# A down projection in seven products instead of eight

## The chip, the cores and the metric

The kernel runs on one core of a Trainium2 chip. A core has TensorE (matrix products, into the PSUM banks), VectorE (DVE), ScalarE (ACT), GpSimd (POOL) and SyncE (SP, which here issues the transfers), each with its own queue, and 16 DMA engines. The metric is the time of one execution on the device in microseconds (us), lower is better. The profile is one execution taken by the hardware profiler.

## The reference

One layer of a streaming encoder for 1024 + 64 = 1088 tokens of width 1024, in float32: token mixers, cross attention, an MLP and a last norm.

```python
x += mix @ w_out
x += cross_attention(rms_norm(x), mem_k, mem_v)
h = rms_norm(x, norm_ffn_g)
x += square(relu(h @ w_up)) @ w_down      # w_up 1024 x 4096, w_down 4096 x 1024
y = rms_norm(x, final_g)
```

This case is about the last two lines. With t = square(relu(h @ w_up)), the down projection multiplies t (1088 x 4096) by w_down and adds the result to x.

## The kernel before

Activations lie transposed, with features on the 128 partitions and tokens along the free axis. A feature block is 128 features, so x has 8, t has 32. To keep float32 accuracy at the faster matmul format, every operand is split into a high part (ACT copies it to the format fp32r) and a low part (DVE subtracts), and each product is three matmuls: high x high, high x low, low x high (`mm3`). `tt` is a two-input operation on DVE, or on POOL where asked; `split_lo` makes the low part.

The **up projection** (`up`) already uses seven products. Two output blocks, the two halves of the inner dimension and the two quarters of a token half form a 2 x 2 x 2 problem; seven products of sums of these (named "1" to "7", done in the order "1562734") replace eight, each of 4 inner blocks x 3 matmuls of 272 columns. A job is one pair of output blocks for one token half (84 matmuls) or both (168). `self.jobs` lists three one-half jobs, thirteen with both halves, and three one-half jobs for the half left out at the start (`LATE = 3`). `pair_units` forms the sums of weights on POOL and splits them; the results of a job are rectified, squared, scaled and stored to a DRAM buffer (`tdram`).

The **down projection** is plain. The 32 blocks of t are taken in eight groups of four (`FBS`); the next group is loaded (`t_load`) and split (`t_split`) while this one is multiplied. For each of the 8 output blocks and each of three token groups, 4 x 3 matmuls go to one PSUM bank, and DVE adds the bank to the residual tile `xr` in SBUF. So every one of the eight groups adds into all of `xr`. The last group is taken by token groups of 416, 416 and 256, each followed by its final norm and stores.

Buffers: 35 slots of 1152 columns shared by nearly everything, three each for raw, high and low weights, eight PSUM banks in two tags of four. Up to the end of the attention a helper (`inorder`) keeps each engine's operations in written order; in the MLP the framework's planner places an operation when by its own estimate its inputs and a buffer are there, in written order among those that are ready. A queue then executes what it was given strictly in order.

Of the kernel before, what the change touches and what calls it, by code (L numbers as in the profile page):

```python
# [23 lines left out]
FB = 4  # L24
NFB = 32 // FB
# [3 lines left out]
NSLOT = 35  # L29
# [11 lines left out]
LATE = 3  # L41
FBS = list(range(2, NFB)) + [1, 0]
# [11 lines left out]
class Trunk:  # L54
    def __init__(self, nc, tc, a, pools):
        self.nc, self.tc, self.a = nc, tc, a
        self.const, self.wp, self.sp, self.tp, self.ps, self.dp = pools
        self.uid = 0
        self.bg = []
        self.seq = {}  # L60
        self.hold = None
        self.consts()
# [11 lines left out]
    def bank(self, tag):  # L74
        return self.ps.tile([P, 512], F32, tag=tag, name=self.name("ps" + tag))
# [5 lines left out]
    def consts(self):  # L81
# [10 lines left out]
        self.masks = c.tile([P, 8, 512], U8, name="masks")  # L92
# [905 lines left out]

    def pair_units(self):

        gp = self.nc.gpsimd
        (_, ri), (_, rj) = self.raws.pop(0), self.raws.pop(0)
        s12, s34 = (self.slot(n="sw")[:, :1024].rearrange("p (k n) -> p k n", k=KT) for _ in range(2))
        self.tt(s12[:, :4], rj[:, :4], rj[:, 4:], ADD, gp)
        self.tt(s12[:, 4:], s12[:, :4], ri[:, :4], SUB, gp)
        self.tt(s34[:, :4], ri[:, :4], rj[:, :4], SUB, gp)
        self.tt(s34[:, 4:], ri[:, 4:], s12[:, 4:], SUB, gp)
        ops = {}
        for src, k0, names in ((ri, 0, "12"), (s12, 0, "56"), (s34, 0, "73"), (rj, 4, "4")):
            hi = self.wp.tile([P, KT, P], F32R, tag="whi", name=self.name("wh"))  # L1010
            lo = self.wp.tile([P, KT, P], F32R, tag="wlo", name=self.name("wl"))
            n = 4 * len(names)
            self.act(hi[:, :n], src[:, k0:k0 + n], AF.Copy)
            self.split_lo(lo[:, :n], src[:, k0:k0 + n], hi[:, :n])
            for j, x in enumerate(names):
                ops[x] = (hi[:, 4 * j:4 * j + 4], lo[:, 4 * j:4 * j + 4])
            if names == "4":
                self.fetch()
                self.fetch()
# [5 lines left out]
    def up(self, ops, units, ready, tdram, side):  # L1025


        jobs = self.jobs
        for n, (p, cs) in enumerate(jobs):
# [3 lines left out]
            for i, m in enumerate(self.ORDER):  # L1033
# [23 lines left out]
                if m in "5273":  # L1057
# [4 lines left out]
                    elif m in "73":  # L1062
                        self.prep()
                if i < len(steps):
                    steps[i]()
            del ops[:4]
            for c in cs:
                self.nc.sync.dma_start(tdram[2 * p:2 * p + 2, :, c * H:c * H + H].rearrange("o p t -> p o t"), st[c][1])

    def mlp(self, o, x1, x2src):  # L1070
        nc = self.nc
        tdram = self.dp.tile([4 * NFB, P, T], F32, name="tt")
        self.jobs = [(p, (0,)) for p in range(LATE)] + [(p, (0, 1)) for p in range(LATE, NPAIR)]
        self.jobs += [(p, (1,)) for p in range(LATE)]
        self.halves, self.accs = [[], []], []
        ready = [{}, {}]
        self.rb = self.two(n="rb")
# [9 lines left out]
        def first():  # L1087
# [5 lines left out]
        unit = lambda: ops.append(next(units))  # L1093
        self.project(0, o[0], x1, x2src, {5: [a], 6: [a, first], 7: [a]})
        self.project(1, o[1], x1, x2src, {0: [a, ra], 1: [ra, a], 2: [a], 3: [a], 4: [a], 5: [a, b], 6: [b, unit],
                                          7: [b, unit]})
        xr, raws, ts = [], {}, {}

        def t_load(fb):
            raws[fb] = []  # L1100
            for f in range(FB):
                t = self.slot(n="t")
                nc.sync.dma_start(t[:, :T], tdram[FB * fb + f])
                raws[fb].append(t)

        def t_split(fb):
            ts.setdefault(fb, []).append(self.hl(raws[fb].pop(0)[:, :T], None))

        def xr_load():
            x = self.slot(n="xr")  # L1110
            nc.sync.dma_start(x[:, :T], x2src[len(xr)])
            xr.append(x)
        f0 = FBS[0]
        sp = lambda: t_split(f0)
        self.up(ops, units, ready, tdram, {
# [232 lines left out]
```

## Time and profile before

| what | value |
|---|---|
| median of 3 runs (lowest, highest) | 1589.76 us (1585.19, 1591.19) |
| profiled execution, its own time | 1591.52 us |
| span of the profile | 1589.7 us |
| PE busy | 1546.3 us (97%) |
| DVE, ACT, POOL busy | 899.9, 578.4, 225.3 us |
| mean granted TensorE clock | 0.982 |

The span is the time from the first to the last instruction. A busy engine sets the time only where others wait for it, so the stretches have to be looked at one by one. Lines name the engine, the line of the code, the operation and the tiles as output<-inputs: `wl<-wr,wh` is the low part of a weight from its raw and high part, `xr<-psd,xr` the addition of a bank to the residual.

### The profile page before, as it was taken

The numbers are of one execution on the slowest core, as the hardware profiler recorded it, in microseconds if no ns is written. First come the engines' busy times: TensorE is split into PE (matmuls) and PEld (weight loads), VectorE is DVE, ScalarE is ACT, GpSimd is POOL, SyncE is SP. The second block draws the span as 40 slices with busy tenths as digits, with TensorE's granted clock in tenths as the row PEclk, the third lists the DMA queues.
The fourth block names the chain that finished last, engine by engine and source line by source line (L and its number), as shares of the span: only waits on it lengthen the run. The fifth ranks groups of instructions, "written<-read, shape, count | busy, mean of one in ns | idle before, by whom it ended". The sixth has DMA issues, their size and how long they took to land.

```text
span 1589.7 us, 24469 instructions
## 1 busy us (share of the span) xinstructions
PE 1546.3 (97%) x10312; PEld 1510.8 (95%) x10312; DVE 899.9 (57%) x1268; ACT 578.4 (36%) x1034; POOL 225.3 (14%) x143
## 2 busy tenths in 40 slices
PE   7899999999999999999998999999989999999997
PEld 7699998899999999989998999999989999999997
DVE  7837868955654433584479444444476444434434
ACT  7711141436252221463455444444353112102124
POOL 2720002200000000000026322222320000000005
PEclk9899999999999999998999999999999999999999
DMA  8421000101013411212542322322376322221103
GB/s 303 160 81 41 27 31 17 36 20 44 28 45 130 153 50 66 80 54 85 177 143 94 108 107 97 110 102 92 108 274 238 124 97 97 72 78 55 53 1 113
DMA packets 54942, 150.60 MB, mean 95 GB/s; under 512 B 6704, under 2 KB 14384, under 8 KB 54832
## 3 DMA queue, kind: packets, MB, share of 16 engines
q1 hardware_dynamic: 51952, 148.37, 26.7%
q8 instruction: 81, 1.33, 0.4%
q10 hardware_dynamic: 2880, 0.66, 0.2%
q14 instruction: 29, 0.24, 0.1%
HBM read 115.11 MB, written 33.91 MB: 94 GB/s over the span
## 4 chain that ended last, share of the span: by engine, by line
PE 64%; issue 26%; DVE 5%; POOL 2%; ACT 1%; DMA 1%; SPq 0%; POOLq 0%; ACTq 0%; DVEq 0%
PE psd L199 46%; PE psm L199 11%; PE psm L536 3%; DVE wl L133 1%; POOL xr L132 1%; DVE cacc L136 1%; POOL sw L132 1%; DMA wr<-w_up 1%; PE psm L614 1%; ACT wh L125 1%; PE psm L616 0%; PE psm L507 0%; DMA wr<-wk 0%; PE psm L625 0%; PE psd L856 0%
## 5 line engine op out<-in xcount | busy, mean ns | idle before, releaser
L199 PE MATMUL psd<-lo,wh 128*128 128x364 f32 (+2 forms) x1632 | 540.6, 331 | 4.2 <-DVE lo L136 4.2
L199 PE MATMUL psd<-hi,wl 128*128 128x364 f32 (+2 forms) x1632 | 541.4, 332 | 3.0 <-DVE wl L133 3.0
L199 PE MATMUL psd<-hi,wh 128*128 128x364 f32 (+2 forms) x1632 | 541.0, 332 | 0.0
L125 ACT ACTIVATE wh<-wr 128x1024 fp32r<-128x1024 f32 (+1 forms) x141 | 138.3, 983 | 495.9 <-PE psd L199 335.1
L199 PEld LDWEIGHTS psd<-lo,wh 128*128 128x128 f32 x1632 | 309.0, 189 | 5.8 <-DVE lo L136 5.5
L199 PEld LDWEIGHTS psd<-hi,wl 128*128 128x128 f32 x1632 | 309.4, 190 | 3.6 <-DVE wl L133 3.2
L199 PEld LDWEIGHTS psd<-hi,wh 128*128 128x128 f32 x1632 | 309.4, 190 | 1.1
L133 DVE TENSOR_TENSOR wl<-wr,wh 128x1024 fp32r<-128x1024 f32 (+1 forms) x141 | 178.1, 1266 | 149.3 <-ACT wh L125 149.3
L133 DVE TENSOR_TENSOR xr<-psd,xr 128x364 f32<-128x364 f32 (+3 forms) x192 | 102.0, 534 | 177.2 <-PE psd L199 177.2
L199 PE MATMUL psm<-th,wh 128*128 128x272 f32 x448 | 131.6, 294 | 4.6 <-ACT wh L125 3.8
L199 PE MATMUL psd<-th,wl 128*128 128x272 f32 x448 | 130.6, 293 | 3.5 <-DVE wl L133 3.5
L199 PE MATMUL psd<-th,wh 128*128 128x272 f32 x448 | 131.0, 293 | 3.0 <-DVE t L133 3.0
L199 PE MATMUL psm<-tl,wh 128*128 128x272 f32 x448 | 130.1, 291 | 0.0
L199 PE MATMUL psm<-th,wl 128*128 128x272 f32 x448 | 130.1, 292 | 0.0
L199 PE MATMUL psd<-tl,wh 128*128 128x272 f32 x448 | 129.9, 290 | 0.0
L199 PEld LDWEIGHTS psm<-th,wh 128*128 128x128 f32 x448 | 85.5, 191 | 5.8 <-ACT wh L125 4.2
L136 DVE SCALAR_TENSOR_TENSOR cacc<-glu,vecs,cacc 128x1118 f32<-128x1118 f32 x60 | 90.5, 1509 | 0.7
L199 PEld LDWEIGHTS psd<-th,wl 128*128 128x128 f32 x448 | 85.4, 191 | 3.7 <-DVE wl L133 3.7
L199 PEld LDWEIGHTS psd<-th,wh 128*128 128x128 f32 x448 | 85.3, 191 | 3.8 <-DVE t L133 3.7
L199 PEld LDWEIGHTS psm<-tl,wh 128*128 128x128 f32 x448 | 85.7, 191 | 0.0
L199 PEld LDWEIGHTS psd<-tl,wh 128*128 128x128 f32 x448 | 85.6, 191 | 0.0
L199 PEld LDWEIGHTS psm<-th,wl 128*128 128x128 f32 x448 | 85.3, 191 | 0.0
(238 smaller groups left out, 2375.9 us busy)
## 6 DMA issues: line engine op xcount, KB each, us to landing
wr<-w_up SPq DMA_DIRECT2D x38, 512.0 KB, 3.3
tt<-t SPq DMA_DIRECT2D x32, 544.0 KB, 2.9
t<-tt SPq DMA_DIRECT2D x32, 544.0 KB, 4.6
wr<-w_down SPq DMA_DIRECT2D x32, 512.0 KB, 3.3
wr<-w_in SPq DMA_DIRECT2D x22, 512.0 KB, 3.2
x<-res SPq DMA_DIRECT2D x16, 544.0 KB, 2.8
wr<-xo SPq DMA_DIRECT2D x16, 512.0 KB, 3.5
x<-xT SPq DMA_DIRECT2D x8, 544.0 KB, 6.6
```

Source lines behind the costliest of these rows:

```text
L125: return self.inorder("act", lambda: self.nc.scalar.activation(out, in_, f, **kw))
L132: return self.inorder("pool", lambda: eng.tensor_tensor(out, a, b, op))
L133: return self.inorder("dve", lambda: self.nc.vector.tensor_tensor(out, a, b, op))
L136: return self.inorder("dve", lambda: self.nc.vector.scalar_tensor_tensor(out, in0, s, in1, op0, op1))
L199: return self.inorder("pe", lambda: self.nc.tensor.matmul(*args, **kw))
L536: mm(pv[:m, c], k[:, c * P:c * P + m], qc[:, :, 1, :], start=True, stop=True)
L614: mm(ps[:w, c * P:c * P + P], sc[:w, s:s + w], vt[:w, s:s + P], start=True, stop=first)
```

## The change

Down becomes a 2 x 2 x 2 problem as well. The two quarters of a token half, two output blocks and the two halves of the inner blocks are combined; seven products per combination. For each token half, four blocks of four pairs of inner blocks; in each, two groups (`dp`) of two pairs of output tiles, so that one product is 2 x 4 x 3 matmuls of 272 columns into two banks. Each of the seven products is followed by one DVE addition of 2 x 272 columns into `xr`.

The sums of t that the products need are made in the up stage: after every job POOL forms four differences of quarters for each half, and they are stored beside t. `t_load` fetches one operand at a time, already summed. The sums of w_down are made on POOL (four of 1024 columns per group), for each token half anew, so w_down is read twice. Five of seven operand splits are on DVE, two on POOL. The first half's final norm runs during the second half's first two blocks. The PSUM pool is closed after up and opened again as four tiles of two banks. `LATE` goes from 3 to 4 (20 jobs, 12 of them with both halves), the slots from 35 to 36, and the weight sums of up are written partly over the raw weights.

```diff
-LATE = 3
+LATE = 4
...
+    def pair_sums(self):
...
         self.tt(s12[:, :4], rj[:, :4], rj[:, 4:], ADD, gp)
         self.tt(s12[:, 4:], s12[:, :4], ri[:, :4], SUB, gp)
-        self.tt(s34[:, :4], ri[:, :4], rj[:, :4], SUB, gp)
-        self.tt(s34[:, 4:], ri[:, 4:], s12[:, 4:], SUB, gp)
+        self.tt(rj[:, :4], ri[:, :4], rj[:, :4], SUB, gp)
+        return ri, rj, s12
...
-                self.nc.sync.dma_start(tdram[2 * p:2 * p + 2, :, c * H:c * H + H].rearrange("o p t -> p o t"), st[c][1])
+                t = st[c][1].rearrange("p o (h t) -> p (o h) t", h=2)
+                self.nc.sync.dma_start(tdram[c, p, :, 0:4], t)
+                d = self.slot(n="d")[:, :4 * Q].rearrange("p (k t) -> p k t", k=4)
+                self.tt(d[:, 0], t[:, 1], t[:, 0], SUB, gp)
+                self.tt(d[:, 2], t[:, 3], d[:, 0], SUB, gp)
+                self.tt(d[:, 1], t[:, 3], t[:, 1], SUB, gp)
+                self.tt(d[:, 3], t[:, 2], d[:, 2], SUB, gp)
+                self.nc.sync.dma_start(tdram[c, p, :, 4:8], d)
...
+    def t_split(self, blk, m):
...
+        self.act(hi, full, AF.Copy)
+        self.tt(lo, full, hi.bitcast(F32), SUB, self.nc.gpsimd if m in "34" else None)
...
+    def quads(self):
...
+                a11, a21 = get(0), get(2)
+                yield
+                a22, a12 = get(3), get(1)
+                yield
+                s1, s2 = (self.slot(n="sw")[:, :1024].rearrange("p (k n) -> p k n", k=KT) for _ in range(2))
+                self.tt(s1, a21, a22, ADD, gp)
+                self.tt(s2, s1, a11, SUB, gp)
+                yield
+                self.tt(a21, a11, a21, SUB, gp)
...
+    def down_units(self):
...
+            for m, src in zip(self.ORDER, (a11, s1, s2, a12, a21, a12, a22)):
...
+                self.act(hi, src, AF.Copy)
+                self.split_lo(lo, src, hi)
+                if m == "2":
+                    self.tt(a12, a12, s2, SUB, self.nc.gpsimd)
+                yield hi, lo
...
+    def down(self, q, loads, splits):
+        units = self.down_units()
+        ops = [next(units), next(units)]
...
+        self.swap_psum()
+        fin = [self.final(c) for c in range(2)]
+        for n, blk in enumerate(self.blocks):
...
+            for dp in range(2):
...
+                    for (a, i, k) in ((0, 0, 0), (0, 0, 1), (0, 2, 2), (0, 4, 3), (0, 6, 4), (1, 2, 5), (1, 3, 6)):
+                        if a == dp:
+                            add(i, self.t_load, nx, self.ORDER[k])
+                    for (a, i, k) in ((0, 2, 0), (0, 4, 1), (0, 6, 2), (1, 0, 3), (1, 2, 4), (1, 4, 5), (1, 6, 6)):
+                        if a == dp:
+                            add(i, self.t_split, nx, self.ORDER[k])
...
+                if n in (NFB, NFB + 1):
+                    for i in range(7):
+                        add(i, next, fin[0], None)
...
+                for i in (0, 1, 3, 4):
+                    add(i, next, q, None)
...
+                for i, m in enumerate(self.ORDER):
...
+                    for pr in range(2):
+                        for k in range(4):
+                            self.mm3(banks[b][:, pr, :Q], wh[:, 4 * pr + k], wl[:, 4 * pr + k], th[:, k], tl[:, k],
+                                     k == 0 and m in "152", k == 3, skip_group_check=m not in "152")
+                    r, h = self.C_AT[m]
+                    x = self.xr[c, dp, r][:, :, h * Q:h * Q + Q]
+                    self.tt(x, banks[b][:, :, :Q], x, ADD)
+                    u = next(units, None)
...
+                    for f in steps[i]:
+                        f()
...
+    def swap_psum(self):
+        self.psx.__exit__(None, None, None)
+        self.psx = self.tc.tile_pool(name="psum2", bufs=4, space=bass.MemoryType.PSUM)
+        self.ps = self.psx.__enter__()
```

Here `mm3` and `split_lo` are unchanged. In `down`, at each product, one further weight unit is split (two products ahead of its use), then the steps listed for that product are done: operand loads and splits for the next block, loads and sums of the next group's weights.

More of the change, by code (lines that the diff above doesn't have):

```diff
@@ L23 @@
 PH = 15
-FB = 4
-NFB = 32 // FB
+NFB = 4
 EPS = 1e-6
@@ L1025, in up @@
     def up(self, ops, units, ready, tdram, side):
-        jobs = self.jobs
-        for n, (p, cs) in enumerate(jobs):
+        gp = self.nc.gpsimd
+        for n, (p, cs) in enumerate(self.jobs):
             cur = ops[0]
@@ L1093, in mlp @@
         unit = lambda: ops.append(next(units))
+        sums = lambda: self.sums.append(self.pair_sums())
         self.project(0, o[0], x1, x2src, {5: [a], 6: [a, first], 7: [a]})
[L1095 to L1104, printed above, removed]
@@ new lines, in mlp @@
+        self.project(1, o[1], x1, x2src, {0: [a, ra], 1: [ra, a], 2: [a], 3: [a], 4: [a], 5: [a, sums], 6: [unit],
+                                          7: [unit, b]})
+        self.blocks = [(c, fb) for c in range(2) for fb in range(NFB)]
+        self.xr = {}
+        self.tq = {}
+        b0 = self.blocks[0]
+        load = [lambda m=m: self.t_load(b0, m) for m in self.ORDER]
+        split = [lambda m=m: self.t_split(b0, m) for m in self.ORDER]
+        x = lambda: self.xr_load(0)
+        q = self.quads()
@@ new lines, in mlp @@
+        qs = lambda: next(q)
+        self.up(ops, units, ready, self.tdram, {
+            0: [[rbb], [b], [rbb], [], [b]], 1: [[b], [], [], [b]], 2: [[b], [], [], [b]],
+            3: [[b], [], [b]],
+            NPAIR: [[load[0]], [], [load[1]], [], [split[0]]],
+            NPAIR + 1: [[load[2]], [], [split[1]], [], [load[3]], [], [split[2]]],
+            NPAIR + 2: [[load[4]], [], [split[3]], [x], [x], [split[4]]],
+            NPAIR + 3: [[x], [x, qs], [qs], [qs], [qs]]})
+        self.down(q, load[5:], split[5:])
@@ new lines, in final @@
+    def final(self, c):
+        nc, gp = self.nc, self.nc.gpsimd
+        accs = []
+        last = c == 1
+        for dp in range(2):
+            sq = [self.two(n="fsq") for _ in range(2)]
+            for r in range(2):
+                self.act(sq[r], self.xr[c, dp, r], AF.Square)
+            self.tt(sq[0], sq[0], sq[1], ADD, None if last else gp)
+            accs += [sq[0][:, 0], sq[0][:, 1]]
+            for r in range(2):
+                for q in range(2):
+                    if not last or r:
+                        x = self.xr[c, dp, r][:, q]
+                        self.act(x, x, AF.Copy, scale=self.vec("final_g", 4 * dp + 2 * q + r))
+            yield
+        r = self.rstd_cols(accs, CT, D, "q")
+        yield
+        ps = self.bank2().rearrange("p a b -> p (a b)")
+        self.bcast_cols(ps, r, CT, 0)
+        rb = self.two(n="frb")[:, 0]
+        self.act(rb, ps[:, :H], AF.Copy)
+        yield
+        for dp in range(2):
+            for r in (1, 0):
+                x = self.xr[c, dp, r]
+                for q in range(2):
+                    o = 4 * dp + 2 * q + r
+                    if last and r == 0:
+                        self.stt(x[:, q], x[:, q], self.vec("final_g", o), ps[:, :H], MUL, MUL)
+                    else:
+                        self.tt(x[:, q], x[:, q], rb, MUL, gp)
+                    nc.sync.dma_start(self.a["o_yT"][o][:, c * H:c * H + H], x[:, q])
+                yield
@@ L1207, in all_weights @@
                 yield "s", a["w_up"][2 * p + j]
-        for fb in FBS:
-            for o in range(4):
-                yield "c", a["w_down"][fb, o]
     def run(self):
```

199 lines of the change are left out of this document (96 added, 103 removed).

## The prediction

> **What bounds the kernel now.** I read the page first, then the busy time by stretch, then the queue of transfers for the pace of one round, then the groups by shape.
>
> ```profile
> span 1589.7 us, 24469 instructions
> PE 1546.3 (97%) x10312; PEld 1510.8 (95%) x10312; DVE 899.9 (57%) x1268; ACT 578.4 (36%) x1034; POOL 225.3 (14%) x143
> DVE  7837868955654433584479444444476444434434
> POOL 2720002200000000000026322222320000000005
> PEclk9899999999999999998999999999999999999999
> ```
>
> TensorE is busy nearly all the time; VectorE and GpSimd look idle over most of the MLP (slices 21 to 40). The stretches of the MLP are: two-half jobs of the up projection, its last three one-half jobs, seven down blocks, the last down block with the end, and (last two rows) the first three one-half jobs of the up projection and the first of them by itself.
>
> ```profile
> 895.00:1145.00 250.00, 250.00 (x1985) 250.00 (x1984) 116.28 (x164) 104.90 (x192) 71.79 (x48) 1.00 0.29 103
> 1152.40:1193.20 40.80, 36.23 (x256) 34.98 (x255) 29.96 (x33) 22.38 (x35) 10.07 (x6) 0.92 0.77 276
> 1192.30:1526.50 334.20, 334.20 (x2018) 334.20 (x2018) 157.48 (x228) 61.66 (x61) 0.00 (x0) 1.00 0.27 97
> 1526.50:1589.70 63.20, 55.16 (x338) 53.52 (x336) 29.37 (x55) 26.38 (x51) 21.10 (x19) 0.94 0.20 71
> 838.00:880.00 42.00, 35.46 (x253) 34.41 (x253) 39.33 (x36) 24.52 (x40) 29.08 (x16) 0.92 0.30 103
> 840.00:862.00 22.00, 17.19 (x112) 16.59 (x111) 21.75 (x17) 12.16 (x21) 19.50 (x11) 0.84 0.21 74
> ```
>
> The columns are length, then busy time and count of PE, weight load, DVE, ACT and POOL, then clock, DMA share and GB/s. In the up jobs and the seven down blocks TensorE is never idle, so matmul time sets the pace, and in the down blocks POOL does nothing at all. The last row is the opposite: DVE is busy 21.75 of 22.00 us, POOL 19.50, and it is TensorE that waits. That row matters below.
>
> **The pace of a matmul.** Transfers repeat once per round:
>
> ```profile
> 942.21 2.58 SPq L1068 DMA_DIRECT2D tt<-t  x2
> 963.40 2.58 SPq L1068 DMA_DIRECT2D tt<-t  x2
> 1254.90 24.22 SPq L159 DMA_DIRECT2D wr<-w_down  x3
> 1302.69 24.22 SPq L159 DMA_DIRECT2D wr<-w_down  x3
> ```
>
> An up job with both halves takes 963.40 - 942.21 = 21.19 us for 2 x 7 x 4 x 3 = 168 matmuls of 272 columns, 0.1261 us each. A down block takes 47.79 us for 8 x 3 x 4 x 3 = 288 matmuls of 364 or 360 columns, 0.1659 us each.
>
> **What the change removes.** Down loses its 8 x 288 = 2304 matmuls and gets 2 halves x 4 blocks x 2 output groups x 7 products x 24 = 2688 of 272 columns, the form of the up jobs. One half block (one output group) is 168 x 0.1261 = 21.2 us on TensorE, a product 3.03 us, and all sixteen are 339 us against 8 x 47.79 = 382. If TensorE alone counts, 43 us are gained.
>
> **What it adds to DVE and POOL.** The durations:
>
> ```profile
> L133 DVE TENSOR_TENSOR xr<-psd,xr 128x364 f32<-128x364 f32 x108 | 57.3, 535 | 97.1 <-PE psd L199 97.1
> L133 DVE TENSOR_TENSOR t<-psm,t 128x272 f32<-128x272 f32 x35 | 15.5, 442 | 21.9 <-PE psm L199 21.9
> L133 DVE TENSOR_TENSOR lo<-t,hi 128x1088 fp32r<-128x1088 f32 x28 | 35.4, 1285 | 5.5 <-ACT hi L125 5.5
> L133 DVE TENSOR_TENSOR wl<-wr,wh 128x1024 fp32r<-128x1024 f32 x27 | 33.0, 1224 | 7.8 <-ACT wh L125 7.8
> L125 ACT ACTIVATE hi<-t 128x1088 fp32r<-128x1088 f32 x28 | 29.5, 1101 | 52.4 <-PE psd L199 47.9 <-DMA t<-tt 4.5
> L125 ACT ACTIVATE wh<-wr 128x1024 fp32r<-128x1024 f32 x27 | 28.6, 1058 | 199.8 <-PE psd L199 199.8
> L136 DVE SCALAR_TENSOR_TENSOR t<-t,rb 128x544 f32<-128x544 f32 x47 | 35.0, 744 | 0.8
> 41.89 2.35 DVE L133 TENSOR_TENSOR wl<-wr,wh 128x1024 fp32r<-128x1024 f32 x2
> ```
>
> Back to back, a weight split takes 2.35/2 = 1.17 us on DVE; an operand split 1.25 by the same small overlap; an addition of two 272-column banks into the residual 0.70 (from 442 ns at 272 columns and 535 at 364, about 1 ns a column: 0.72 at 544). A block of two output groups has 14 weight splits (before: 4), 14 additions and 5 of the 7 operand splits on DVE: 14 x 1.17 + 5 x 1.25 + 14 x 0.70 = 32.4 us in the 42.4 us of TensorE. ACT has 14 x 1.06 + 7 x 1.10 = 22.5 us, which stays hidden. DVE too would be hidden, were it alone. But POOL, idle here before, now gets 8 sums of 1024 columns and two operand splits of 1088 per block. What happens when DVE and POOL work together is seen early in the kernel:
>
> ```profile
> 21.76 2.55 POOL L132 TENSOR_TENSOR sq<-sq,sq 128x1088 f32<-128x1088 f32 x1 [20.79 <-ACT sq L125]
> 50.62 24.60 POOL L132 TENSOR_TENSOR x<-x,rb 128x1088 f32<-128x1088 f32 x7 [14.13 <-ACT rb L125]
> 53.04 9.30 DVE L133 TENSOR_TENSOR wl<-wr,wh 128x1024 fp32r<-128x1024 f32 x3 [1.17 <-ACT wh L125]
> 62.26 3.63 DVE L136 SCALAR_TENSOR_TENSOR lo<-x,vecs,hi 128x1088 fp32r<-128x1088 f32 x1
> 65.82 3.50 DVE L133 TENSOR_TENSOR wl<-wr,wh 128x1024 fp32r<-128x1024 f32 x1
> 845.50 0.78 DVE L133 TENSOR_TENSOR t<-psd,t 128x272 f32<-128x272 f32 x2
> ```
>
> Seven POOL multiplies take 24.60 us, 3.51 each instead of 2.55, and a DVE weight split among them 3.50 instead of 1.17. They take turns: 3.51 is one operation of each. So a 1088-column POOL operation holds up a DVE operation with two SBUF inputs by 3.51 - 1.2 = 2.3 us, and one of 1024 columns by 2.16. The additions from PSUM are not held up (0.78 for two, in the stretch of the last row above where POOL was busy).
>
> The Trainium skill, "SBUF — State Buffer", section "Who interferes with whom", calls this an exclusive lock under which the loser fully blocks; by that a turn would be 2.55 + 1.17 = 3.72 us, which is 0.2 us more than the trace has and would add about 2 us a block (14 us in all) to the sum; I go by the trace.
>
> So a block has 14 x 1.17 + 5 x 1.25 = 22.6 us of such work on DVE and 8 x 2.16 + 2 x 2.3 = 21.9 on POOL. That is 44.5 us if everything else fits beside it, and 54.3 if the 9.8 us of additions never run beside POOL; TensorE needs 42.4. Between them I take 49.4: of ten POOL operations about seven start right behind a weight split that an addition follows (14 of the 19 splits), and each such addition, 0.70 us, runs beside POOL: 54.3 - 4.9. Laid out in order, a half block gives the same: the difference a12 - s2 follows the split of the fourth product's weights, the three sums for the next group take turns with the splits behind it, the sixth split ends 18.0 us into the half block, TensorE had been done with the fifth product at 15.2, and the half block ends after 24.4 us. This lies near the stretch 840 to 862, where DVE is full and TensorE has 17.19 of 22.00.
>
> Down then is 7 blocks x 49.4 = 345.8, and the last block, without next operands and nearly without sums, 42.4. The two POOL splits of the first block fall at its start (2 x 2.3, less 1.0 beside additions: 3.6), and the first half's closing norm puts 2 additions of 1088 and 8 products of 544 on POOL (2 x 2.3 + 8 x 1.15 = 13.8, less 4.9: 8.9) into the fifth and sixth block. The end, once the last product is done, by rows of this size: addition 0.7, square 1.1, sum 1.3, column sums and roots 2.1, reciprocals 0.4, spreading 1.4, copy 0.6, four POOL products of 544 columns 5.5, last store 2.5, together 15.6. Sum 416.3 us. Before, the same stretch was 1589.70 - 1192.30 = 397.4. So **+18.9 us**; its ends are -15.4 (44.5 a block) and +59 (54.3, nothing beside POOL).
>
> **The up stage.** POOL gets four differences of 272 columns per half and job, and SP a second store that waits for them; behind that store stand the next weights, asked for half a job later, so I price no wait there. In a two-half job DVE has 4.2 us of weight splits, 2.6 of rectifying (744 ns rows) and 2.3 of additions, and is held up by four sums and eight differences:
>
> ```profile
> 819.68 1.29 POOL L132 TENSOR_TENSOR sw<-wr,wr 128x512 f32<-128x512 f32 x1
> 842.15 2.27 POOL L132 TENSOR_TENSOR sw<-wr,wr 128x512 f32<-128x512 f32 x1
> 844.39 2.32 POOL L132 TENSOR_TENSOR sw<-sw,wr 128x512 f32<-128x512 f32 x1
> ```
>
> 844.39 - 842.15 = 2.24 us per turn, less 1.2 of DVE, is 1.05 for 512 columns and about 0.6 for 272: 4.2 + 4.8 on top of 9.1 is 18.1 of 21.2 us, hidden. A one-half job has 10.6 us of TensorE and 6.6 + 4.2 + 2.4 = 13.2 on DVE, 2.6 too many, and there are now eight such jobs, not six. The last ones also carry five operand splits (6.3) and the first sums for down (8.6), less 4.2 as the very last job prepares no up weights: 8 x 2.6 + 6.3 + 8.6 - 4.2 = 31.5, and 29 with some additions beside POOL. Before, 40.8 us held three such jobs (31.8) and 1.3 of down: 7.7 lost; and at the first jobs 42.00 - 35.46 = 6.5. So **+15 us**, between 0 (the differences wait while TensorE runs ahead) and +25.
>
> **The change of PSUM pools.** Before, the first down matmuls were mixed among the last up product; the new pool can open only when the old banks are read out, and the first split waits behind that: 0 to 5 us, I take **+3**. DMA: a half block moves about 4.1 MB, 166 GB/s over 24.7 us, and 276 GB/s went through at share 0.77 (second row of the stretches), so it is hidden; 36 slots are tight where the halves change, which I do not price.
>
> **Sum.** The profiled execution took 1591.5 us (span 1589.7 and 1.8 around it): 1591.5 + 18.9 + 15 + 3 = 1628.4. The median of the runs, 1589.8, is 1.8 lower: **1627 us**, slower by 2.3%.
>
> **Rivals.**
>
> *TensorE sets the pace after all: faster.* POOL's sums slip into the times when DVE waits for a product, and each delay stays under the two products that the weights are ahead. Then down is 8 x 42.4 + 15.6 = 354.8, 42.6 less than before; with +3 for the rest 1552, or 1550 beside the median. For it: DVE alone needs 32.4 of 42.4 us. Against it: 44.5 us of turns do not fit in 42.4; it decides for this case if a POOL sum costs DVE under about 1 us.
>
> *Turns packed without loss: same.* 44.5 a block, all additions beside POOL: 397.4 - 15.4 + 15 + 3 gives 1594, or 1592. For it: DVE can work ahead. Against: five operand splits directly follow a weight split.
>
> *The clock falls too: slower still.* A half block leaves TensorE idle 2.8 us in one piece.
>
> ```profile
> 1176.65 0.29 PE L199 MATMUL psm<-th,wl 128*128 128x272 f32 x1
> 1180.53 0.60 PE L199 MATMUL psm<-th,wh 128*128 128x272 f32 x1 [3.59 <-ACT wh L125]
> 1181.15 0.43 PE L199 MATMUL psm<-th,wh 128*128 128x272 f32 x1
> 1181.38 0.43 PE L199 MATMUL psm<-tl,wh 128*128 128x272 f32 x1
> 1186.59 0.32 PE L199 MATMUL psm<-th,wl 128*128 128x272 f32 x1
> 1186.74 0.29 PE L199 MATMUL psm<-th,wh 128*128 128x272 f32 x1
> ```
>
> After 3.6 us without work the matmuls come every 0.23 us instead of 0.126 for some 6 us, about 25 of them: 2.6 us lost. Fourteen half blocks of that are +36: 1663. Against it: the wait is shorter than the one that did this.
>
> The Trainium skill, "TensorE: Matmul & The Clock Gate", section "Part 1: The HAM clock gate (the "warmup" mystery)", lets the clock fall only after an idle window of about 3.4 us; by that 2.8 us would cost nothing and this rival would be out, and the trace's 3.59 us agrees with it but does not bound it from below.
>
> **How the numbers follow.** Forecast 0.55, TensorE bound 0.15, packed turns 0.18, clock 0.12. About 0.5% is what a measurement here can tell from no change: under 1582 is faster, over 1598 slower. The TensorE-bound case and a quarter of the packed one are faster (0.20), most of the rest of the packed one with a little of the forecast is the same (0.14), what is left slower (0.66). The range leaves out the TensorE-bound case and the top of the clock case: 1575 to 1675. The forecast's own is 1600 to 1660.
>
> **What would show it.** Right: DVE and POOL together above 95% busy or waiting in the down blocks, weight splits on DVE at 2 to 3.5 us where a POOL sum runs, TensorE waiting on DVE for the split that precedes the sixth product, a block near 49 us. Wrong: blocks at 42.4 us with TensorE never idle, or TensorE waiting on DMA or on slots instead.

## The result, and the profile after

| | before | after | predicted |
|---|---|---|---|
| median (lowest, highest), us | 1590.47 (1585.19, 1591.68) | 1692.95 (1687.64, 1694.23) | 1627, range 1575 to 1675 |
| after/before, 95% interval | | 1.0645 (1.0611 to 1.0678) | 1.023 |
| span of the profile, us | 1589.7 | 1691.7 | |
| PE, DVE, ACT, POOL busy, us | 1546.3, 899.9, 578.4, 225.3 | 1553.0, 1131.3, 682.7, 608.6 | |
| mean granted TensorE clock | 0.982 | 0.953 | |

The kernel became slower, as forecast, but by 102 us instead of 37, and the time lies above the range. Three lines of the page of after, in forty slices of the span:

```profile
DVE  7829869766554335846776666666579878877863
...
POOL 2710013000000000001376666665577645685451
PEclk9799999999999999999989999998888989989997
```

Up to slice 20 little has changed. From the up stage on POOL works in half of the time and more, where before it showed 2 to 3 tenths in up and nothing in down, and in the down stage (from slice 29) the granted clock is below 0.9 in five slices before the end, where before none was.

Where the 102 us are is read at two boundaries: the last matmul of the up projection and the last product. The stretch ahead of the MLP differs by up to 6 us between profiles (the matmul named next starts last at 712.2 to 718.0), though its code is the same, so the up stage is measured from a matmul just ahead of it, the last `psm<-kvh,lo`. The groups by tile, with first and last start, before:

```profile
L199 PE MATMUL psm<-kvh,lo x72: 274/283/365, 664.6 to 717.0; 128*128 128x256 f32 x64, 128*64 128x256 f32 x8
```

and after:

```profile
L202 PE MATMUL psm<-kvh,lo x72: 274/283/364, 663.2 to 716.7; 128*128 128x256 f32 x64, 128*64 128x256 f32 x8
L202 PE MATMUL psm<-th,wl x448: 283/290/594, 896.1 to 1217.7; 128*128 128x272 f32 x150
```

Before, the last `psm<-th,wl` starts at 1193.1, so that this part took 476.1 us; after it takes 1217.7 - 716.7 = 501.0, **24.9 more**. Down's first product follows at 1218.5; the last one starts at 1667.6, 449.1 us later. Before, the first matmuls of down are mixed among the last of up; from the prediction's boundary at 1192.3 to the last product at 1579.4 it is 387.1: **62.0 more**. From the last product to the end of the span it is 24.1 us against 10.3: **13.8 more**.

The down stage of after by blocks, each from the last addition into `xr` of the block before to its own last (the first block from its first addition): the first block, the third, the fifth (with the first half's norm) and the seventh. Columns as in the prediction's stretches.

```profile
1221.84:1285.47 63.63, 48.48 (x335) 46.67 (x336) 50.68 (x34) 27.52 (x27) 48.29 (x19) 0.89 0.65 225
...
1339.94:1396.09 56.15, 48.28 (x336) 47.43 (x335) 44.41 (x34) 21.44 (x22) 30.46 (x10) 0.88 0.47 157
...
1452.79:1517.42 64.63, 52.95 (x380) 51.94 (x379) 48.87 (x36) 26.67 (x31) 49.10 (x19) 0.87 0.52 178
...
1571.22:1625.51 54.29, 46.38 (x338) 45.56 (x337) 40.69 (x32) 20.59 (x21) 29.28 (x11) 0.94 0.35 111
```

A steady block takes 54 to 57 us, not 49.4. No engine is full: in the steady blocks shown DVE is busy 40.7 of 54.3 and 44.4 of 56.2 us. TensorE needs 42.4 us of matmuls at full clock and shows 46 to 48, since part of them runs at the lower clock; the rest it waits. For whom, in the down stage of after (total, times, longest):

```profile
PE psq L202 <- DVE xr L136: 37.3, 14, 8.3
PE psq L202 <- DVE wl L136: 17.6, 13, 2.5
PE psq L202 <- ACT wh L128: 14.8, 8, 6.2
```

```profile
ACT wh L128 <- PE psq L202: 103.7, 50, 6.6
ACT wh L128 <- POOL wr L135: 100.3, 15, 10.6
```

TensorE waits mostly for a bank to be added up (`xr`), ACT waits 100 us for POOL. One such place in order of time, the second output group of the third block:

```profile
1368.71 2.41 POOL L135 TENSOR_TENSOR sw<-wr,wr 128x1024 f32<-128x1024 f32 x1 [13.35 <-DMA wr<-w_down]
1371.19 3.26 POOL L135 TENSOR_TENSOR wr<-wr,wr 128x1024 f32<-128x1024 f32 x1
1374.41 3.39 POOL L135 TENSOR_TENSOR sw<-sw,wr 128x1024 f32<-128x1024 f32 x1
1377.77 3.52 POOL L135 TENSOR_TENSOR tl<-tl,th 128x1088 fp32r<-128x1088 f32 x1
1381.25 2.40 POOL L135 TENSOR_TENSOR wr<-wr,sw 128x1024 f32<-128x1024 f32 x1
...
1383.68 2.95 ACT L128 ACTIVATE wh<-wr 128x1024 fp32r<-128x1024 f32 x3 [6.64 <-POOL wr L135]
...
1384.77 2.42 DVE L136 TENSOR_TENSOR wl<-wr,wh 128x1024 fp32r<-128x1024 f32 x1 [5.24 <-ACT wh L128]
...
1387.24 0.60 PE L202 MATMUL psq<-th,wl 128*128 128x272 f32 x1 [1.94 <-DVE wl L136]
```

The difference a12 - s2 (`wr<-wr,sw`), which the running group needs for its sixth product, stands on POOL behind the three sums of the next group and an operand split. Those sums could not start before their weights had landed (13.35 us idle), and with 1024 columns in 2.4 to 3.5 us each the difference is done only at 1383.65. ACT's copy waits for it 6.64 us, DVE's split behind ACT 5.24, TensorE behind DVE. ACT and DVE execute in order, so the additions of the banks queue up behind the late split as well. That is only a part of the 37.3 us against `xr`: in most of these waits DVE had been at work without a pause, with splits of up to 3.4 us ahead of the addition, and with turns alone (below) 26.9 us of it are still there.

### The profile page after: what moved, and what is told of

It reads as the page before. It is cut to its first block, busy times and chain, and to the rows that moved or that the text cites. A ratio compares the mean times of both kernels' runs of the same rounds, so it can differ in the third digit from the quotient of the medians.

```text
span 1691.7 us, 26082 instructions
## 1 busy us (share of the span) xinstructions
PE 1553.0 (92%) x10752; PEld 1506.9 (89%) x10752; DVE 1131.3 (67%) x1280; ACT 682.7 (40%) x1137; POOL 608.6 (36%) x350
## 4 chain that ended last, share of the span: by engine, by line
PE 64%; DVE 13%; issue 8%; POOL 8%; DMA 4%; ACT 2%; SPq 0%; POOLq 0%; DVEq 0%; ACTq 0%
PE psd L202 41%; PE psm L202 10%; PE psq L202 6%; DVE wl L136 6%; POOL sw L135 3%; PE psm L539 3%; DVE tl L136 2%; POOL wr L135 2%; ACT wh L128 2%; DMA wr<-w_down 2%; DMA wr<-w_up 1%; DVE xr L136 1%; POOL xr L135 1%; POOL d L135 1%; DVE cacc L139 1%
## 5 line engine op out<-in xcount | busy, mean ns | idle before, releaser
L136 DVE TENSOR_TENSOR wl<-wr,wh 128x1024 fp32r<-128x1024 f32 (+1 forms) x233 | 342.8, 1477 | 155.3 <-ACT wh L128 155.1
L202 PE MATMUL psq<-th,wh 128*128 128x272 f32 x896 | 273.7, 305 | 52.6 <-DVE xr L136 37.3
L202 PE MATMUL psd<-lo,wh 128*128 128x364 f32 (+1 forms) x912 | 304.1, 333 | 3.3 <-DVE lo L139 3.3
L202 PE MATMUL psd<-hi,wl 128*128 128x364 f32 (+1 forms) x912 | 304.2, 334 | 3.0 <-DVE wl L136 3.0
L202 PE MATMUL psd<-hi,wh 128*128 128x364 f32 (+1 forms) x912 | 304.6, 335 | 0.0
L202 PE MATMUL psq<-th,wl 128*128 128x272 f32 x896 | 271.8, 304 | 17.6 <-DVE wl L136 17.6
L202 PE MATMUL psq<-tl,wh 128*128 128x272 f32 x896 | 269.8, 301 | 0.0
L202 PEld LDWEIGHTS psq<-th,wh 128*128 128x128 f32 x896 | 180.7, 202 | 57.8 <-issue 30.1
L202 PEld LDWEIGHTS psq<-th,wl 128*128 128x128 f32 x896 | 180.3, 201 | 20.5 <-DVE wl L136 20.5
L202 PEld LDWEIGHTS psq<-tl,wh 128*128 128x128 f32 x896 | 180.8, 202 | 0.0
L202 PE MATMUL psd<-th,wh 128*128 128x272 f32 x448 | 133.1, 297 | 12.5 <-ACT wh L128 7.4
```

The lines of the kernel that those rows point to most:

```text
L136: return self.inorder("dve", lambda: self.nc.vector.tensor_tensor(out, a, b, op))
L202: return self.inorder("pe", lambda: self.nc.tensor.matmul(*args, **kw))
```

## The experiments

Two theories at the start. **Turns**: DVE loses what POOL's operations take from it, wherever their results go, and the block price was too low. **Waits on POOL**: what is behind POOL in a chain (ACT, DVE, TensorE) waits for POOL's results in the order in which POOL got them, and the turns are the smaller part.

Six of the variants were executed once each: those without the sums, with the sums unread, with turns alone, with another order, without the differences and with the later store. The first three and the one without the differences leave out part of the computation. A stage of the same code is not the same to the microsecond in two kernels: up took 501.0 to 505.7 us in the six profiles that have after's up stage, and down 449.1, 444.6 and 437.1 in the three that differ in up alone. The shares below are good to about that.

### The weight sums left out

```diff
-                self.tt(s1, a21, a22, ADD, gp)
-                self.tt(s2, s1, a11, SUB, gp)
-                self.tt(a21, a11, a21, SUB, gp)
...
-            for m, src in zip(self.ORDER, (a11, s1, s2, a12, a21, a12, a22)):
+            for m, src in zip(self.ORDER, (a11, a21, a22, a12, a21, a12, a22)):
...
-                if m == "2":
-                    self.tt(a12, a12, s2, SUB, self.nc.gpsimd)
```

> The changed kernel, but in the down stage the four weight sums per group are left out (the products take the raw weight blocks in their place, so the output is not the reference's). All else, the two operand splits on POOL too, stays. Theory T (turns: POOL's sums hold up DVE's splits): DVE keeps 32.4 of the 42.4 us that TensorE needs for a block, so a block falls from 53.6 to 43 to 44 us and the whole to about 1692 - 8 x 10 = 1612. Theory O (order: a product waits for a sum that stands late in POOL's queue, behind sums for the next group that wait for their weights): the same, 1605 to 1615. Theory D (the weights arrive late, whatever POOL does): a block stays at 50 or more, 1670.

Measured: 1606.18 us (before beside it 1588.91). Down, from first to last product, takes 356.9 us instead of 449.1, and a steady block is TensorE alone:

```profile
1310.66:1353.03 42.37, 42.37 (x338) 42.37 (x337) 35.17 (x34) 21.76 (x22) 5.07 (x2) 1.00 0.57 192
1395.41:1454.44 59.03, 52.59 (x388) 52.02 (x387) 40.59 (x37) 27.57 (x31) 24.42 (x11) 0.91 0.57 200
```

So transfers, buffers, banks, DVE's other work and the two operand splits left on POOL (5.07 us) carry a block at TensorE's pace. All 92 us that down loses beyond it come with the four sums (and the two slots that these take in each group). The whole fell by 87 us, as up took 505.3 us here. The block at the change of halves (second row) still takes 59.03 us, 16.7 more than the others, without any sum.

### The sums made, but read by nobody

```diff
-                self.tt(a21, a11, a21, SUB, gp)
+                self.tt(s1, a11, a21, SUB, gp)
...
-            for m, src in zip(self.ORDER, (a11, s1, s2, a12, a21, a12, a22)):
+            for m, src in zip(self.ORDER, (a11, a21, a22, a12, a21, a12, a22)):
...
-                    self.tt(a12, a12, s2, SUB, self.nc.gpsimd)
+                    self.tt(s2, a12, s2, SUB, self.nc.gpsimd)
```

> The same POOL sums as the changed kernel, of the same size at the same places, but written to the two scratch tiles only; the products take the raw weight blocks, so nothing waits for a sum (the output is not the reference's). Theory T: DVE is held up as before, a block stays at 49 to 53 us, 1660 to 1690. Theory O: the waits are gone, what is left is TensorE and a DVE that is held up in part, 44 to 46 us, 1620 to 1635. The difference of this run to the one without sums is what taking turns costs by itself.

Measured: 1686.3 us, down 446.2. This did not tell the theories apart, though it looks as if turns alone did it all. The sums read the raw weights and write slots, so these stay taken until POOL is done, and in this kernel ACT waits for the slots:

```profile
ACT th L128 <- POOL sw L135: 64.3, 10, 10.3
```

No product reads a sum here, yet the chain still hangs on POOL, through buffers instead of data.

### Turns alone

The kernel without weight sums, and per group four POOL additions of 1024 columns on a constant tile, started by a one-column operation on the group's weights. They hold no buffer of the chain.

```diff
+                if self.scr is None:
+                    self.scr = self.slot(n="scr")[:, :1024]
+                self.tt(self.scr[:, 0:1], a21[:, 0, 0:1], a22[:, 0, 0:1], ADD, gp)
+                rb = self.masks_f[:, :1024]
+                for _ in range(4):
+                    self.tt(self.scr, rb, rb, ADD, gp)
```

> As the run without weight sums, but POOL does four additions of 1024 columns per group on a constant tile into one scratch tile, once the group's weights have come; nothing reads them and no buffer waits for them (the output is not the reference's, as the products take raw weights). This is the turn-taking alone. Theory T as forecast: 49 us a block, 357 + 7 x 6.5 = 400 us of down, 1650 in all. If turns cost what POOL's lengthened operations take (3.3 us each, 8 a block, all on DVE's path): 53 us, 1685. If most of the loss came by the buffers that POOL's sums hold: 44 to 46 us, 1620.

Measured: 1639.85 us (before beside it 1586.30), down 398.5. So POOL's operations as such cost 398.5 - 356.9 = 41.6 us, and 449.1 - 398.5 = 50.6 us come from what is behind POOL. The stand-ins are a little shorter than the sums (2.55 us in the mean of the stage, the sums 2.98), so the 41.6 may be somewhat low; DVE's weight splits are held up alike, 1.86 us in the mean in both. A steady block, and then two waits of the same length and what followed them:

```profile
1329.00:1374.96 45.96, 43.03 (x340) 42.64 (x339) 42.68 (x35) 22.13 (x22) 28.40 (x12) 1.00 0.54 177
...
1387.30:1391.30 4.00, 3.95 (x19) 3.98 (x20) 3.87 (x3) 0.00 (x0) 1.02 (x1) 0.57 0.59 161
1341.60:1345.60 4.00, 3.94 (x31) 3.97 (x32) 4.00 (x4) 0.04 (x1) 1.03 (x1) 1.00 0.62 156
```

```profile
1341.66 0.36 PE L203 MATMUL psq<-th,wh 128*128 128x272 f32 x1 [2.18 <-DVE xr L137]
...
1387.35 0.36 PE L203 MATMUL psq<-th,wh 128*128 128x272 f32 x1 [2.10 <-DVE xr L137]
...
1388.30 0.43 PE L203 MATMUL psq<-th,wl 128*128 128x272 f32 x1
1388.52 0.43 PE L203 MATMUL psq<-th,wh 128*128 128x272 f32 x1
```

With only two operand splits a block behind POOL (TensorE waits for one of them once, 5.5 us in the first block) a steady block takes 46.0 us, close to the 44.5 of turns packed without loss. After the wait of 2.18 us that ends at 1341.66 the clock is 1.00 over the next 4 us; after the slightly shorter one that ends at 1387.35 it is 0.57, and some 14 matmuls come every 0.226 us instead of 0.126.

The trace has each change of the clock with its time, and that tells why. In each of the thirteen traces all changes lie on one grid of 3.413 us, to within 0.01 us. By the windows of this grid, the two places are:

```profile
1339.95:1343.37 3.42, 1.71 (x14) 1.74 (x15) 3.42 (x3) 0.50 (x1) 2.68 (x1) 1.00 0.42 120
...
1384.33:1387.74 3.41, 1.31 (x11) 1.12 (x10) 3.41 (x4) 1.06 (x1) 3.33 (x2) 1.00 0.10 12
1387.74:1391.15 3.41, 3.41 (x17) 3.41 (x17) 3.41 (x3) 0.00 (x0) 0.58 (x1) 0.50 0.55 170
1391.15:1394.56 3.41, 3.41 (x29) 3.41 (x28) 1.97 (x3) 1.06 (x1) 0.00 (x0) 1.00 0.95 274
```

The wait of 2.10 us lies whole in one window, in which TensorE is busy 1.31 us; the next window runs at half the clock, and the one after it at full again. The wait of 2.18 us is divided by a boundary at 1339.95, and TensorE is busy 1.71 us in the window where it ends. So what counts in these traces is the work within a fixed window and not the length of one wait. Over all thirteen, 2461 windows of the MLP (from 800 us on) start at full clock and hold only matmuls of 272 columns or none. With 0.126 us for a matmul, the 124 that were followed by half the clock had 1.99 us or more without one, and the other 2337 had 1.99 us or less.

That is why time is lost to the clock as well. From the starts of the matmuls in the timeline, the length of down splits into idle time (two starts over 0.5 us apart), matmuls that come 0.2 to 0.3 us after the one before (counted with what they take above 0.126), the first half's small norm matmuls, and 339 us of matmuls at full clock (2688 x 0.126). What is missing to the sum, up to 4 us, are shorter pauses.

| kernel | down, us | idle | lower clock | norm |
|---|---|---|---|---|
| without weight sums | 356.9 | 7.9 | 4.5 | 5.2 |
| turns alone | 398.5 | 37.8 | 15.2 | 5.2 |
| sums made, unread | 446.2 | 75.0 | 22.9 | 5.4 |
| after | 449.1 | 75.6 | 26.5 | 5.2 |

### The order of the sums

The first sum of the next group is issued only after a12 - s2 of the running one.

```diff
-                self.tt(s1, a21, a22, ADD, gp)
+                if self.last_a12 is None:
+                    self.tt(s1, a21, a22, ADD, gp)
+                else:
+                    with self.after(self.last_a12):
+                        self.tt(s1, a21, a22, ADD, gp)
...
-                    self.tt(a12, a12, s2, SUB, self.nc.gpsimd)
+                    self.last_a12 = self.tt(a12, a12, s2, SUB, self.nc.gpsimd)
```

> The changed kernel with one edge more: POOL may begin the sums for the next group only after the difference a12 - s2 of this group. Work, buffers and results are unchanged. Theory T: no change, block 53 us, 1685 to 1695. Theory O: the split of the product 3 no longer waits behind the next group's sums, ACT and DVE lose 5 to 8 us less per half block and TensorE 2 to 3, a block 48 to 50, 1650 to 1665.

Measured: 1672.68 us, between the two ranges expected; down 424.0. The wait of ACT for the difference falls from 100.3 us to

```profile
ACT wh L129 <- POOL wr L136: 24.7, 7, 8.3
```

and steady blocks take 47 to 53 us, the second to fourth 53.1, 50.7 and 47.3. (Of the 24.7 us, 21.7 are still for the difference.) So the order in POOL's queue is worth 25.1 of the 50.6 us of down; the whole fell by 20.3, as up took 505.7 us here. The other 25.5 were not split up further: data that comes late from the sums and buffers that come free late are both in it.

### All sums and operand splits of down on DVE

```diff
-        self.tt(lo, full, hi.bitcast(F32), SUB, self.nc.gpsimd if m in "34" else None)
+        self.tt(lo, full, hi.bitcast(F32), SUB)
...
-                self.tt(s1, a21, a22, ADD, gp)
-                self.tt(s2, s1, a11, SUB, gp)
+                self.tt(s1, a21, a22, ADD)
+                self.tt(s2, s1, a11, SUB)
...
-                self.tt(a21, a11, a21, SUB, gp)
+                self.tt(a21, a11, a21, SUB)
...
-                    self.tt(a12, a12, s2, SUB, self.nc.gpsimd)
+                    self.tt(a12, a12, s2, SUB)
```

> The changed kernel with all work of the down stage that POOL had (8 weight sums and 2 operand splits per block) on DVE. DVE then has 32.4 + 8 x 1.17 + 2 x 1.25 = 44.3 us per block against 42.4 on TensorE, and nothing takes turns but the first half's norm. Theory T: a block at 45 to 47 us, 1692 - 8 x 7.5 = 1625 to 1640. Theory O: the sums still come late in an in-order queue, now DVE's own, and the additions stand behind them: 49 to 53 us, 1665 to 1700.

Measured: 1618.64 us, ratio 1.0177 (1.0146 to 1.0207), down 370.8. A steady block:

```profile
1317.10:1360.43 43.33, 42.77 (x336) 42.48 (x336) 42.74 (x44) 21.84 (x23) 0.00 (x0) 1.00 0.54 188
```

DVE is full, does all that two engines did before, and a block takes 43.3 us instead of 54 to 57. Made by DVE, a sum costs it 1.2 us. Made by POOL, it takes POOL 2.3 to 3.5 us and still costs DVE about 1.2: DVE's splits in down take 280.6 us in after and 204.1 without the sums, 76.5 more for 64 sums.

### The up stage: no differences, and a later store

First the differences of quarters left out, with t stored a second time in their place; then the differences as they are, but their store issued one job later, behind the next request for weights.

```diff
-                d = self.slot(n="d")[:, :4 * Q].rearrange("p (k t) -> p k t", k=4)
-                self.tt(d[:, 0], t[:, 1], t[:, 0], SUB, gp)
-                self.tt(d[:, 2], t[:, 3], d[:, 0], SUB, gp)
-                self.tt(d[:, 1], t[:, 3], t[:, 1], SUB, gp)
-                self.tt(d[:, 3], t[:, 2], d[:, 2], SUB, gp)
-                self.nc.sync.dma_start(tdram[c, p, :, 4:8], d)
+                self.nc.sync.dma_start(tdram[c, p, :, 4:8], t)
```

> The changed kernel without the four POOL differences per half and job in the up stage; the second store stays and writes t itself in their place, so the output is not the reference's. The forecast put about 20 us of the up stage on the delay of DVE by these differences in the one-half jobs. Theory T (turns): the down stage then starts some 20 us earlier than at 1218.5 us, 1670 in all. Theory Q (queue: the store of the differences stands in SP's queue ahead of the next up weights, and waits for POOL): the store no longer waits, and it is 25 us earlier, at the 1192 us of the kernel before. If neither, the eight one-half jobs themselves cost it: at 1210 or later.

```diff
-                self.nc.sync.dma_start(tdram[c, p, :, 4:8], d)
+                held.append((c, p, d))
...
+                if m == "2":
+                    flush()
```

> The changed kernel, but the store of a job's differences is issued one job later, behind the request for the next up weights; POOL's work is unchanged. Theory Q: the up stage gets back most of its 25 us, the down stage starts at 1195 to 1203 us, 1670 to 1678 in all. Theory T: no change, 1216 to 1219 and 1690.

Measured: 1658.78 us without differences, 1676.06 with the later store. The last matmul of up, first without the differences and then with the later store:

```profile
L202 PE MATMUL psm<-th,wl x448: 284/290/554, 888.1 to 1196.4; 128*128 128x272 f32 x150
```

```profile
L202 PE MATMUL psm<-th,wl x448: 285/290/428, 897.0 to 1206.0; 128*128 128x272 f32 x150
```

The marks ahead of the MLP are 713.9 and 717.5, so up takes 482.5 and 488.5 us, where after takes 501.0 and before 476.1. The differences cost 18.5 us, and 12.5 of it is only the place of their store in SP's queue. The queue near the end of up in after shows how:

```profile
1165.75 0.43 SPq L1143 DMA_DIRECT2D tl<-tt  x1
1179.52 0.32 SPq L1086 DMA_DIRECT2D tt<-d  x1
1179.93 0.38 SPq L162 DMA_DIRECT2D wr<-w_up  x1
```

The store waits for POOL almost 14 us and the next weights stand right behind it; they start 0.4 us after it. The remaining 6.4 us of up (482.5 - 476.1) were not taken apart.

### A version with the pieces together

The sums on DVE and the later store, and at the end the second half's squares folded to one tile (10 column sums on TensorE instead of 40) with six of the last eight products on DVE:

```diff
+            if last:
+                self.tt(sq[0][:, 0], sq[0][:, 0], sq[0][:, 1], ADD)
+                if accs:
+                    self.tt(sq[0][:, 0], sq[0][:, 0], accs.pop(), ADD)
+                accs.append(sq[0][:, 0])
...
-                    if last and r == 0:
+                    if last and (r == 0 or dp):
```

> All weight sums and operand splits of down on DVE, the store of the differences one job later, and a shorter end: the squares of the second half are summed to one tile, so that the column sums take 10 matmul records and not 40, and six of the eight last products go to DVE, two to POOL. The results are the reference's. By the run with all on DVE (1618.6) less 17 to 22 for the up stage by theory Q and 7 for the end: 1590 to 1595, the same as the kernel before within 0.5%; by theory T for the up stage 1610.

Measured: 1600.88 us, ratio 1.0093 (1.0071 to 1.0115), 6 us above the expectation. Then every POOL operation that is left in the MLP on DVE too, up's weight sums and the differences among them (the line below in each of the functions; two differences for the first operands stay on POOL):

```diff
-        gp = self.nc.gpsimd
+        gp = None
```

> The version with the sums on DVE, the late store and the short end (e7_dve_late_store_end), and beside that every remaining POOL operation of the MLP on DVE: up's weight sums, the differences of quarters, the first half's closing squares and products (only two differences of the first operands stay on POOL). Nothing is left out of the computation. If taking turns is what a POOL operation costs DVE, then a one-half up job needs 6.6 + 4 x 0.62 + 4 x 0.4 = 10.7 us on DVE alone instead of 13.2 with turns, beside 10.6 of TensorE, a two-half job 14.8 of 21.2, so the up stage gives back most of the 10 us that it still loses, and the first half's norm 7.8 instead of 13.8: about 1588 us (1583 to 1596), the same as before. The rival, that POOL's work in the up stage is hidden and the loss there comes from queues and buffers, expects no change from e7_dve_late_store_end or a little slower, since DVE gets 0.6 + 0.4 us a job half more: 1600 to 1606.

Measured: 1579.00 us, ratio **0.9944** (0.9923 to 0.9966): faster than the kernel before by 0.6%, and 9 us better than expected. Up takes 1185.2 - 712.7 = 472.5 us, 3.6 less than before in spite of the differences and their stores; down 367.3, 19.8 less; the end 19.9, 9.6 more.

That left open whether the new down projection has any part in the gain, as up's weight sums, on POOL in the kernel before as well, had been moved too. So only those were moved, in the kernel before, with its plain down projection:

```diff
     def pair_units(self):
-        gp = self.nc.gpsimd
+        gp = None
```

> The kernel before with one edit: the four sums of up weights per pair of output blocks are made on DVE instead of POOL. The down projection stays plain. It tells how much of the gain of e9_mlp_on_dve lies in the up stage alone. There the down start moved from 1192.3 us in the kernel before to about 1186, and in the window of the first one-half jobs (838 to 880) PE was busy 36.57 us instead of 35.46. If that is from the sums' turns with DVE, this kernel gains the same 4 to 7 us: ratio 0.996 to 0.997. If the gain needs the new down projection, it stays within 0.2% of before.

Measured: 1578.03 us, ratio **0.9936** (0.9917 to 0.9955). One edit of one line in the old kernel gives the same as the whole new scheme at its best. The first one-half jobs of up (before: PE 35.46 and DVE 39.33 of 42.00, clock 0.92; the stretch is taken 4.8 us earlier, as the mark ahead of the MLP is), and the tile view:

```profile
833.20:875.20 42.00, 37.13 (x279) 35.39 (x279) 40.74 (x53) 26.95 (x45) 5.65 (x3) 1.00 0.33 116
```

```profile
L199 PE MATMUL psm<-kvh,lo x72: 274/283/364, 659.8 to 712.2; 128*128 128x256 f32 x64, 128*64 128x256 f32 x8
...
L199 PE MATMUL psm<-th,wl x448: 282/290/394, 869.7 to 1178.7; 128*128 128x272 f32 x150
```

Up takes 466.5 us instead of 476.1. These 9.6 us are nearly all of the 11.0 by which the medians differ; what follows up took 397.1 us, before 396.6. Whether turns or waits for POOL's sums cost the 9.6 us was not separated. Last, the first half's squares folded as well, in the version with everything on DVE:

```diff
-            if last:
-                self.tt(sq[0][:, 0], sq[0][:, 0], sq[0][:, 1], ADD)
+            self.tt(sq[0][:, 0], sq[0][:, 0], sq[0][:, 1], ADD)
...
-            else:
-                accs += [sq[0][:, 0], sq[0][:, 1]]
```

> e9_mlp_on_dve with the squares of the first half's norm folded to one tile on DVE before the column sums on TensorE, as the second half does already: 10 column-sum matmuls at the change of halves instead of 40, and three DVE additions of 544 columns (0.72 us each) more. In e9_mlp_on_dve the block at the change of halves takes 55.73 us with 51.77 of TensorE, against 43.3 and 42.8 in the steady block: some 9 us of small matmuls. If they are what the change of halves costs, 30 fewer of them save about 4 to 6 us, less up to 2.2 on DVE: 2 to 4 us faster than e9_mlp_on_dve. If DVE sets the pace there (50.4 of 55.7 busy), nothing is gained or 2 us are lost.

Measured: 1577.94 us, ratio 0.9937 (0.9917 to 0.9957), not to be told from 1579.00. The block at the change of halves went from 55.73 to 54.89 us. Before the fold and with it:

```profile
1368.84:1424.57 55.73, 51.77 (x386) 50.70 (x386) 50.42 (x57) 31.65 (x38) 0.00 (x0) 0.94 0.61 205
```

```profile
1372.18:1427.07 54.89, 48.35 (x356) 46.61 (x356) 51.99 (x59) 31.67 (x38) 0.00 (x0) 0.97 0.61 208
```

TensorE has 3.4 us less to do there, DVE 1.6 more, and the time hardly moves: the small matmuls are not what the change of halves costs. What does was not settled.

## Why the prediction was wrong

The direction was right and the list of places too; the sum came out 66 us short. By its terms:

- **Down, 400.7 us forecast ahead of the end, 449.1 measured (+48.4).** The step that failed is "Between them I take 49.4". It counted the time that DVE and POOL take from each other, with the operations "laid out in order": "the difference a12 - s2 follows the split of the fourth product's weights". On POOL it followed the three sums of the next group instead, which had to wait for a transfer, since the planner orders by its own estimate of when an input is there, as the description of the kernel had said. The order alone is 25.1 us, all that hangs on POOL's results and buffers 50.6. A price by busy time could not contain it: it is a latency through four engines in order. That the steady blocks lie near the forecast's upper end of 54.3 is chance: that end was for turns, and with turns alone a block takes 46.0.
- **The price of a turn was too high, and its sum met the measured one by luck.** The forecast has every POOL sum hold up DVE by 2.16 us. Whole turns happen (the longest weight split in after's down stage is 3.42 us), but the mean split is 1.86 (206.3 us for 111), and a sum costs DVE 1.2. So the steady block with turns alone is 46.0 us, near the rival of packed turns. Turns alone still gave 398.5 us, beside 400.7 forecast, because the first block (58.8 from its first addition) and the one at the change of halves (58.5) were dearer than the forecast's 53 and 54, and a part of these is the clock.
- **The clock.** The forecast left it out, as a rival of 0.12 at +36 us for the down stage. It came to 26.5 us in down, and 15.2 with turns alone. The reason against that rival, "the wait is shorter than the one that did this", fell: 2.10 us was enough in one place, as it lay whole in one window.
- **The Trainium skill on the clock** ("TensorE: Matmul & The Clock Gate", "Part 1: The HAM clock gate (the "warmup" mystery)"): the prediction took from it that 2.8 us would cost nothing. The trace disagrees: after 2.10 us without a matmul the clock was 0.57 over 4 us, and 2.18 us elsewhere cost nothing. The section also says that the window is free-running. The traces agree: in all thirteen the changes lie on a grid of 3.413 us, and some 2.0 us without a matmul within one window were enough.
- **The up stage, +15 and +3 forecast, 24.9 and 0.8 measured.** The step that failed is "behind that store stand the next weights, asked for half a job later, so I price no wait there": that place is 12.5 us. The change of PSUM pools left 1218.5 - 1217.7 = 0.8 us between up and down, where before, by the same boundary, down began 0.8 ahead of up's end: 1.6 us, not 3.
- **The end, 15.6 forecast, 24.1 measured.** "Column sums and roots 2.1" was the most mis-sized term. In the timeline of after:

```profile
1669.78 1.29 DVE L136 TENSOR_TENSOR fsq<-fsq,fsq 128x1088 f32<-128x1088 f32 x1 [1.18 <-ACT fsq L128]
...
1671.13 6.65 PE L202 MATMUL psq<-ones,fsq 128*128 128x1 f32 x36 [2.95 <-DVE fsq L136]
...
1678.44 2.60 PE L202 MATMUL psq<-ident,rc 128*128 128x128 f32 x10 [0.66 <-DVE rc L237]
```

36 matmuls of one column take 6.65 us, 0.18 each, and the ten that spread the roots 2.60 instead of 1.4. The clock is 0.50 here, from 1669.90 to the end. At full clock, in the kernel before, eight such matmuls take 0.95 us and come every 0.112 us:

```profile
1671.13:1677.78 6.65, 6.65 (x36) 6.55 (x36) 0.00 (x0) 0.04 (x1) 0.00 (x0) 0.50 0.00 0
```

```profile
1547.46 0.95 PE L199 MATMUL psm<-ones,facc 128*128 128x1 f32 x8
```

By these rows 36 would take an estimated 4.0 us at full clock, about twice the forecast's term, and the fallen clock adds the other 2.6. From the last POOL product to the end of the span it is 4.7 us, not 2.5.

- **A slip that changed nothing.** The packed rival's sum is written as "397.4 - 15.4 + 15 + 3"; its 1594 follows from the whole, 1591.5, in place of the down stage's 397.4.

Right were: TensorE at 42.4 us a block as the floor (42.37 without the sums), POOL as the cause (without its sums the 92 us are gone), that DVE and POOL hold each other up, and DMA as no bound by bandwidth (share 0.35 to 0.65). The rival in which TensorE sets the pace after all would have needed POOL's sums below 1 us of DVE; they cost 1.2, closer to it than the forecast's 2.16. What no step considered is that DVE can make the sums itself: 8 x 1.17 more on top of 32.4 and two operand splits of 1.25 is 44.3 us by the prediction's own rows, less than any of its prices for sharing, and it measured 43.3.

The Trainium skill, "SBUF — State Buffer", section "Who interferes with whom", says why POOL's sums are not free for DVE: a DVE operation with two SBUF inputs contends with a POOL operation that reads SBUF, and the contention is an exclusive lock. The trace agrees in kind: a weight split took 1.22 us with POOL idle (35.1 us for 29, in the stretch 1317 to 1404 with the sums on DVE) and 1.86 in the mean with POOL adding constants beside it (206.6 us for 111).

## What to carry to other kernels

Work on a second engine that shares a resource with the busy one is not free because that engine is idle: price it on the busy engine both ways, shared and done there outright, before anything else. When a result passes through several in-order queues, write down what stands ahead of it in each queue, the transfers included; a sum of busy times is only a floor. And before crediting a new scheme with a gain, apply its helpful side edits to the old one: here a single line of it was worth as much as all the rest.

## What was not expected of the hardware

- The granted clock went by fixed windows of 3.413 us: in the MLP, 1.99 us or more without a matmul within one window, together or in pieces, halved it for the next. A wait of 2.10 us did so and one of 2.18, divided by a boundary, did not. Such a window cost 14 x 0.1 = 1.4 us.
- POOL's sums of 1024 columns, 2.3 us at best, took up to 3.5 beside a busy DVE, so the turns stretch both engines. In the kernel before, up's sums on POOL cost the up stage 9.6 us although POOL was busy only 14% of the span.
- A matmul of one column is hardly cheaper than a wide one: 0.112 us from start to start at full clock, beside 0.126 for 272 columns.
